# The opening of a fused attention and convolution block on one core: where the norm weights are loaded, the order of ScalarE's casts, and the order of V's first two token tiles

## The chip, the core and the metric

The kernel runs on one core of a Trainium2 chip. The metric is the device time of one execution in microseconds. Each number of the profile belongs to a single profiled execution.

The engines have short names here, as in the profile: PE is TensorE (matrix products and transposes), PEld its weight loads, DVE is VectorE, ACT is ScalarE, POOL is GpSimd, and SP is SyncE, which in this kernel only issues DMAs. Each engine takes its instructions in the order in which they stand on it.

## What is computed

One layer of a hybrid decoder block on 1024 tokens of width 1024, all in float32:

```python
h = rms_norm(x, attn_norm_w[l])
proj = h @ w_in[l]
q, k, v, u, g = jnp.split(proj, splits, axis=-1)
...
a = diff_attention(q[0], q[1], k[0], k[1], v, lam, rel_bias)
y_a = (rms_norm(a, subln_w[l]) * (1.0 - lam_init)).reshape(B, S, ATTN_WIDTH) @ w_proj_attn[l]
c = causal_depthwise_conv(u_a * jax.nn.sigmoid(u_b), conv_w[l], conv_b[l])
y_b = jax.nn.silu(layer_norm(c, conv_ln_w[l], conv_ln_b[l])) @ w_proj_conv[l]
g_a, g_b = jnp.split(jax.nn.sigmoid(g + gate_b[l]), 2, axis=-1)
x = x + (g_a * y_a + g_b * y_b) @ w_out[l]
h = rms_norm(x, ffn_norm_w[l])
gt, up = jnp.split(h @ w_gate_up[l], 2, axis=-1)
x = x + (jax.nn.silu(gt) * up) @ w_down[l]
```

This case is about the first 60 us: the first `rms_norm`, the transposes that bring its result into the form that PE needs, and the first columns of `h @ w_in`.

## The kernel before

**Split products.** PE works in a format of shorter mantissa. So every float32 operand is split into a high part (a cast, `split_hi`, ACT, L120) and a low part (the operand less its high part, `split_lo`, DVE, L125), and a product is three matmuls: high by high, low by high, high by low. `hT_hi` and `hT_lo` are the two parts of the normalised, transposed x: 8 channel blocks (k = 0 to 7) by 1024 tokens.

**The opening, by token tiles.** A token tile is 128 tokens, i = 0 to 7. For each of them:

- `xload` (L189) fetches its two halves g = 0, 1 of 512 channels, 256 KB each.
- `squares_of` (ACT, L652) forms the sums of squares. Tile 0 goes its own way in `x_first`: one half's squares on ACT, the other's on DVE.
- `roots` turns sums into 1/rms: a first step on DVE (L646), the square root on ACT (L616), then five small steps on DVE (L617 to L621).
- `scale_x` (DVE, L667) multiplies each half by 1/rms and by the norm weights `wb`. These are `attn_norm_w`, broadcast to 128 partitions by two DMAs of 256 KB (L194).
- `turn_x` (PE, L673) transposes a half, four transposes into a PSUM buffer of two; `hi_x` (ACT, L120) and `lo_x` (DVE, L125) put it into `hT_hi` and `hT_lo`.

**V's weights.** 512 columns of V come in four pieces k = 0 to 3 of 512 KB (`v_load`, L821), each with two channel blocks. `w_hi(k)` (ACT) and `w_lo(k)` (DVE) split them. Indices 4 and 5 of the same helpers are the weights of the first U columns, whose two buffers are those of V's pieces 0 and 1, so `u_load` (L828) waits for `w_lo(0)` and `w_lo(1)`. `v_terms` (PE, L688) issues the matmuls of a token tile: 24 of 128x512, namely 8 channel blocks by three products, into one PSUM bank `o`. `TERMS` goes through the blocks with three products each; `halves[g]` are the eight products of four blocks with the weights' high part. `v_out` casts and splits the sum (ACT, DVE) and stores both parts.

**What sets the order.** Where `in_order(...)` stands around a block, each named engine runs the instructions of the block in the order of the program text. There is one such block for V's token tile 0, one for tile 1, one for tile 2, and then blocks for the first U columns. Outside them a planner may move instructions ahead, and does so with the loads and splits of later weights. Here the text's order on an engine matters: an instruction that waits holds up all behind it on its engine. Before the change the norm weights go out on ACT's DMA queue, while x and V's weights go out on SP's. At most eight of these DMAs are under way; a ninth waits for the first to land.

**After the opening** come the rest of V, U, Q, K and the gates with the depthwise convolution on DVE beside them, the attention, the projections, and the channel mixer.

Of the kernel before, what the change touches and what calls it, by code (L numbers as in the profile page):

```python
# [57 lines left out]
def kernel(  # L58
# [27 lines left out]
    nc = tc.nc  # L86
# [25 lines left out]
    def nm(s):  # L112
        uid[0] += 1
        return f"{s}_{uid[0]}"

    def f32(ap):
        return ap.bitcast(F32)

    def split_hi(dst, src):
        act.copy(dst, src)  # L120
# [3 lines left out]
    def split_lo(dst, src, hi):  # L124
        last_lo[0] = dve.tensor_tensor(dst, src, f32(hi), op=ALU.subtract).ins  # L125
# [13 lines left out]
    def pg():  # L139
        npg[0] += 1  # L140
        p_, tag = pgs[npg[0] % len(pgs)]
        return p_.tile([P, 512], F32, tag=tag, name=nm("pg"))
# [48 lines left out]
    xload(0, 0)  # L191
    xload(0, 1, nc.scalar)
    for g in range(2):
        nc.scalar.dma_start(  # L194
            wb[:, 512 * g : 512 * (g + 1)], attn_norm_w[:, 512 * g : 512 * (g + 1)].to_broadcast([P, 512])
        )

# [485 lines left out]
    def v_terms(o, terms, w, i, first, last):  # L683

        ts = slice(i * P, (i + 1) * P)
        for n_, (k, a_, b_) in enumerate(terms):
            l_, r_ = (hT_hi, hT_lo)[a_][:, k, ts], w[k // 2][b_][:, k % 2, :]
            last_mm[0] = pe.matmul(  # L688
                o[:], l_, r_, start=first and n_ == 0, stop=last and n_ == len(terms) - 1
            ).ins  # L690

    def v_out(j, i, o):
        vh = ap.tile([P, 512], F32R, tag="vh", name=nm("vh"))
        vl = ap.tile([P, 512], F32R, tag="vl", name=nm("vl"))
        split_hi(vh[:], o[:])
        split_lo(vl[:], o[:], vh[:])
        for src, dst in ((vh, v_hi[j]), (vl, v_lo[j])):
            nc.sync.dma_start(dst[i * P : (i + 1) * P, :], f32(src[:]))

    TERMS = [(k, a_, b_) for k in range(NKT) for a_, b_ in ((0, 0), (0, 1), (1, 0))]  # L700
# [113 lines left out]
    def opening():  # L814


        raws = [wraw(), wraw()] + [ap.tile([P, 1024], F32, tag="vraw", name=nm("vraw"), bufs=2) for k in range(2)]
        uraw = [wraw(), wraw()]

        def v_load(k):  # L820
            nc.sync.dma_start(  # L821
                raws[k][:].rearrange("p (k c) -> p k c", c=512),
                win[2 * k * P : 2 * (k + 1) * P, V0 : V0 + 512].rearrange("(k p) c -> p k c", p=P),
            )

        def u_load(z):
            c0 = (U0 + D, U0)[z]
            nc.sync.dma_start(  # L828
                uraw[z][:].rearrange("p (k c) -> p k c", c=P),
                win[:, c0 : c0 + P].rearrange("(k p) c -> p k c", p=P),  # L830
            )

        def x_load(i):
            for g in range(2):
                xload(i, g)

        tiles = [vtiles() for k in range(4)] + [wtiles() for z in range(2)]
        raw6 = raws + uraw

        def w_hi(k):  # L840
            split_hi(tiles[k][0][:], raw6[k][:])

        def w_lo(k):
            split_lo(tiles[k][1][:], raw6[k][:], tiles[k][0][:])

        w = [[t_[:].rearrange("p (k c) -> p k c", c=512) for t_ in tiles[k]] for k in range(4)]
        uw = [[t_[:].rearrange("p (k c) -> p k c", c=P) for t_ in tiles[4 + z]] for z in range(2)]
        E_ = mybir.EngineType
        R, PT_ = {}, {}

        def turn_x(i, g):
            PT_[i, g] = x_turn(i, g)

        def hi_x(i, g):
            x_place(i, g, PT_[i, g], False)

        def lo_x(i, g):
            x_place(i, g, PT_[i, g], True)

        def squares_of(i, n):  # L860
            ss = sm.tile([P, 2], F32, tag="ss", name=nm("ss"))
            for e in range(n):
                x_squares(i + e, ss[:, e : e + 1])
            return ss

        def roots(i, n, ss):
            r = rstd_of(ss[:, :n], n, 1.0 / D)
            for e in range(n):
                R[i + e] = r[:, e : e + 1]

        def scale_x(i):
            for g in range(2):
                x_scale(i, R[i], g)

        with in_order(E_.PE, E_.Activation, E_.DVE, E_.SP):
            v_load(0)
            v_load(1)
            x_load(1)
            v_load(2)
            v_load(3)  # L880
            for i in range(2, NT):
                x_load(i)
            R[0] = x_first()
            scale_x(0)
            w_hi(0)
            turn_x(0, 0)
            hi_x(0, 0)
            turn_x(0, 1)
            lo_x(0, 0)
            w_hi(1)  # L890
            hi_x(0, 1)
            lo_x(0, 1)
            w_lo(0)
            ss = squares_of(1, 1)
            w_lo(1)
            u_load(0)
            u_load(1)
            roots(1, 1, ss)
            w_hi(2)
            scale_x(1)  # L900
            w_hi(3)
            w_lo(2)
            w_lo(3)
            o = pg()
            halves = [[(k, a_, 0) for a_ in range(2) for k in range(4 * g, 4 * g + 4)] for g in range(2)]
            v_terms(o, halves[0], w, 0, True, False)
            v_terms(o, halves[1], w, 0, False, False)
            v_terms(o, [(k, 0, 1) for k in range(4)], w, 0, False, False)
            turn_x(1, 0)
            hi_x(1, 0)  # L910
            lo_x(1, 0)
            turn_x(1, 1)
            ss = squares_of(2, 2)
            hi_x(1, 1)
            lo_x(1, 1)
            v_terms(o, [(k, 0, 1) for k in range(4, 8)], w, 0, False, True)
            roots(2, 2, ss)
            scale_x(2)
            v_out(0, 0, o)
        yield  # L920
        with in_order(E_.PE, E_.Activation, E_.DVE, E_.SP):
            o = pg()
            v_terms(o, TERMS[:12], w, 1, True, False)
            for g in range(2):
                turn_x(2, g)
                hi_x(2, g)
                lo_x(2, g)
            scale_x(3)
            w_hi(4)
            ss = squares_of(4, 2)  # L930
            v_terms(o, TERMS[12:], w, 1, False, True)
            roots(4, 2, ss)
            v_out(0, 1, o)
        yield
        with in_order(E_.PE, E_.Activation, E_.DVE, E_.SP):
            o = pg()
            v_terms(o, TERMS[:12], w, 2, True, False)
            for g in range(2):
                turn_x(3, g)
                hi_x(3, g)  # L940
                lo_x(3, g)
            w_lo(4)
            scale_x(4)
            w_hi(5)
            w_lo(5)
            ss = squares_of(6, 2)
            v_terms(o, TERMS[12:], w, 2, False, True)
            roots(6, 2, ss)
            scale_x(5)
            v_out(0, 2, o)  # L950
        yield

        def norm_of(i, nxt):
            for g in range(2):
                turn_x(i, g)
                hi_x(i, g)
                lo_x(i, g)
            if nxt is not None:
                scale_x(nxt)

        sg = {}

        def u_half(z, sb, amid):
            o = gemm_T(uw[z], hT_hi, hT_lo, sb, amid)
            if z == 0:
                sg[sb] = wp.tile([P, 512], F32, tag="sg", name=nm("sg"), bufs=2)
                act.activation(sg[sb][:], o[:], AF.Sigmoid)
            else:
                dve.tensor_tensor(sg[sb][:], o[:], sg[sb][:], op=ALU.mult)
                nc.sync.dma_start(u_d[0][:, sb * 512 : (sb + 1) * 512], sg[sb][:])  # L970

        with in_order(E_.PE, E_.Activation, E_.DVE):
            u_half(0, 0, lambda: norm_of(4, 6))
            norm_of(5, 7)
        yield
        with in_order(E_.PE, E_.Activation, E_.DVE):
            u_half(1, 0, lambda: norm_of(6, None))
            norm_of(7, None)
        yield
        with in_order(E_.PE, E_.Activation, E_.DVE):  # L980
            u_half(0, 1, None)
            vectors()
        yield
        with in_order(E_.PE, E_.Activation, E_.DVE):
            u_half(1, 1, None)
        bg.add([conv_load(0)])
        bg.add(conv_taps(0))
        yield
        yield from v_item(0, w, 3)
# [365 lines left out]
    for c in range(NE, NKT):  # L1355
        w = ws.next()
# [6 lines left out]
    for cl in ((0, 1, 2), (3, 4), (5, 6), (7,)):  # L1363
        pair = [(c, ws.next()) for c in cl]
        for sb in range(2):
            cs = slice(sb * 512, (sb + 1) * 512)
            for c, w in pair:
                g = gated(g_d[NKT + c], cs)
                ya = bp.tile([P, 512], F32, tag="ya", name=nm("ya"), bufs=4)
                nc.sync.dma_start(ya[:], ya_d[c][:, cs])  # L1370
                o = gemm_T(w, cT_hi, cT_lo, sb)
# [61 lines left out]
    for z, (c, ls) in enumerate(WO):  # L1433
        ts_ = [4 * l + i for l in ls for i in range(4)]
        o = {t_: wo_bank(t_) for t_ in ts_}
# [321 lines left out]
```

## Time and profile before

| | |
|---|---|
| time, median of 3 runs (lowest, highest) | 1768.91 us (1768.19, 1770.76) |
| the profiled execution: time, span from first to last instruction | 1769.82 us, 1768.0 us |
| PE busy | 1740.1 us, 98% of the span |
| DVE busy | 1273.1 us, 72% |
| ACT busy | 800.8 us, 45% |
| DMA | 275.29 MB, mean 156 GB/s |

A row of the timeline gives start and length in us, the engine, the line of the program, the operation, what it writes and reads, and how many instructions are merged into the row; in brackets stands how long the engine sat idle before and what ended that. In the names, `px` is the PSUM buffer of the transposes, `pg` that of products, `xt` a token tile of x, `anw_b` the norm weights, `vwh`/`vwl` V's split weights, `whi`/`wlo` other split weights, `xj` the squares' throw-away output, `vh`/`vl` the split V.

### The profile page before, as it was taken

Reading aid. Unit: us, or ns where it says so; the run is one execution under the profiler, and the core shown is the slowest. Engines: PE = TensorE matmul, PEld = TensorE weight load, DVE = VectorE, ACT = ScalarE, POOL = GpSimd, SP = SyncE. Lnnn points to the kernel's source line nnn. Section 1 sums busy time; section 2 is a strip of 40 time slices with the busy share of each in tenths; the row PEclk is TensorE's granted clock in tenths of the full one; section 3 lists DMA queues with packets and bytes.
Section 4 is the critical chain, followed back from the end, with each engine's and each line's share of the span. In section 5 each row is a group of like instructions: output and inputs, shape, how many; then the busy total and the mean of one; then the engine's idle time right before and its main releaser. Section 6 shows DMA issues by size and latency. Waiting matters only on the chain.

```text
span 1768.0 us, 25005 instructions
## 1 busy us (share of the span) xinstructions
PE 1740.1 (98%) x8983; PEld 1484.6 (84%) x8983; DVE 1273.1 (72%) x2171; ACT 800.8 (45%) x1883; POOL 19.6 (1%) x92
## 2 busy tenths in 40 slices
PE   6999999999999999999999999999999999999999
PEld 5778898998999998987788888878888888888887
DVE  6598888998898888885677534867667666665544
ACT  5221141557767776754457313633333333333332
POOL 0000000000000000000000000000000000000000
PEclk9999999999999999999999999999999999999999
DMA  6337334235443244341973544224544544697663
GB/s 231 107 125 232 131 111 115 70 104 138 120 141 105 82 125 145 97 147 60 339 261 108 167 166 143 90 90 152 171 159 148 177 153 148 202 357 250 214 214 131
DMA packets 251110, 275.29 MB, mean 156 GB/s; under 512 B 16505, under 2 KB 166050, under 8 KB 250986
## 3 DMA queue, kind: packets, MB, share of 16 engines
q1 hardware_dynamic: 249130, 267.47, 47.0%
q0 software_dynamic: 1280, 4.91, 0.9%
q10 hardware_dynamic: 576, 1.31, 0.3%
q8 instruction: 71, 1.16, 0.3%
q14 instruction: 53, 0.43, 0.1%
HBM read 176.59 MB, written 78.68 MB: 144 GB/s over the span
## 4 chain that ended last, share of the span: by engine, by line
PE 91%; DMA 3%; DVE 2%; ACT 2%; issue 1%; SPq 0%; DVEq 0%; ACTq 0%
PE acc L1611 19%; PE pg L153 14%; PE pg L154 14%; PE pg L155 14%; PE acc L497 12%; PE pg L688 4%; PE sc L1053 2%; PE sc L1052 2%; PE pT L1088 2%; PE wo L154 2%; PE wo L153 2%; PE wo L155 2%; PE pW L155 1%; PE pW L153 1%; PE pW L154 1%
## 5 line engine op out<-in xcount | busy, mean ns | idle before, releaser
L569 DVE SCALAR_TENSOR_TENSOR acc<-u,cw,acc 128x1024 f32<-128x1024 f32 x240 | 306.9, 1279 | 2.9
L153 PE MATMUL pg<-hT_hi,whi 128*128 128x512 f32 x512 | 201.7, 394 | 0.5 <-ACT hT_hi L120 0.2
L154 PE MATMUL pg<-hT_lo,whi 128*128 128x512 f32 x512 | 200.9, 392 | 0.0
L155 PE MATMUL pg<-hT_hi,wlo 128*128 128x512 f32 x512 | 200.7, 392 | 0.0
L120 ACT CAST whi<-wraw 128x1024 fp32r<-128x1024 f32 x101 | 106.1, 1051 | 182.9 <-PE pg L154 99.5
L125 DVE TENSOR_TENSOR wlo<-wraw,whi 128x1024 fp32r<-128x1024 f32 x101 | 123.0, 1219 | 63.3 <-ACT whi L120 59.4
L125 DVE TENSOR_TENSOR wlo<-draw,whi 128x1024 fp32r<-128x1024 f32 x75 | 91.8, 1224 | 89.1 <-ACT whi L120 86.1
L153 PE MATMUL pg<-whi,hT_hi 128*128 128x256 f32 x512 | 146.0, 285 | 0.3 <-ACT jk L756 0.3
L155 PE MATMUL pg<-whi,hT_lo 128*128 128x256 f32 x512 | 145.8, 285 | 0.0
L154 PE MATMUL pg<-wlo,hT_hi 128*128 128x256 f32 x512 | 145.5, 284 | 0.0
L120 ACT CAST whi<-draw 128x1024 fp32r<-128x1024 f32 x75 | 79.1, 1055 | 129.5 <-PE acc L497 122.6
L1059 ACT ACTIVATE E<-E,mn 128x256 f32<-128x256 f32 (+7 forms) x128 | 99.6, 780 | 45.9 <-DVE mn L1054 44.7
L497 PE MATMUL acc<-wlo,whi 128*128 128x512 f32 x308 | 119.8, 389 | 0.0
L497 PE MATMUL acc<-whi,wlo 128*128 128x512 f32 x308 | 119.8, 389 | 0.0
L153 PEld LDWEIGHTS pg<-hT_hi,whi 128*128 128x128 f32 x512 | 96.2, 188 | 20.5 <-ACT sgg L603 0.7
L155 PEld LDWEIGHTS pg<-hT_hi,wlo 128*128 128x128 f32 x512 | 96.2, 188 | 19.1
L154 PEld LDWEIGHTS pg<-hT_lo,whi 128*128 128x128 f32 x512 | 96.2, 188 | 19.0 <-issue 0.6
L153 PEld LDWEIGHTS pg<-whi,hT_hi 128*128 128x128 f32 x512 | 97.7, 191 | 2.2 <-ACT jk L756 1.0
L154 PEld LDWEIGHTS pg<-wlo,hT_hi 128*128 128x128 f32 x512 | 97.7, 191 | 1.3
L155 PEld LDWEIGHTS pg<-whi,hT_lo 128*128 128x128 f32 x512 | 97.7, 191 | 0.4
L1611 PE MATMUL acc<-h_hi,whi 128*128 128x512 f32 x240 | 93.4, 389 | 0.0
L1611 PE MATMUL acc<-h_lo,whi 128*128 128x512 f32 x240 | 93.4, 389 | 0.0
(280 smaller groups left out, 4191.1 us busy)
## 6 DMA issues: line engine op xcount, KB each, us to landing
wraw<-in_w_gate_up_dram SPq DMA_DIRECT2D x44, 512.0 KB, 4.8
wraw<-in_w_in_dram SPq DMA_DIRECT2D x38, 512.0 KB, 4.2
qs<-qs SPq DMA_DIRECT2D x96, 128.0 KB, 2.3
wd<-in_w_down_dram SPq DMA_DIRECT2D x44, 256.0 KB, 3.2
tdT<-wd SPq DMA_DIRECT2D x88, 128.0 KB, 4.5
draw<-sdS SPq DMA_DIRECT2D x44, 256.0 KB, 2.6
draw<-tdT SPq DMA_DIRECT2D x44, 256.0 KB, 4.3
wraw<-in_w_in_dram SPq DMA_DIRECT2D x32, 256.0 KB, 3.4
```

What stands on the lines that cost most here:

```text
L120: act.copy(dst, src)
L125: last_lo[0] = dve.tensor_tensor(dst, src, f32(hi), op=ALU.subtract).ins
L153: pe.matmul(o, lh, rh, start=start, stop=False)
L154: pe.matmul(o, lh, rl, start=False, stop=False)
L155: last_mm[0] = pe.matmul(o, ll, rh, start=False, stop=stop).ins
L497: m = pe.matmul(o[s_][i][:], l_[:, ts], r_[:, 512:], start=start and j + y_ == 0, stop=j == n - 1 and y_ == 2, skip_group_check=not start,)
L569: dve.scalar_tensor_tensor(acc[0][:], us[c][:, t : t + S], cw[:, c, t : t + 1], acc[0][:], op0=ALU.mult, op1=ALU.add)
L688: last_mm[0] = pe.matmul(o[:], l_, r_, start=first and n_ == 0, stop=last and n_ == len(terms) - 1).ins
L1052: pe.matmul(o[:, :w], qh[:, qs], k, start=True, stop=False)
L1053: last_mm[0] = pe.matmul(o[:, :w], ql[:, qs], k, start=False, stop=True).ins
L1059: act.activation(e[:, :nk], e[:, :nk], AF.Exp, bias=mn[:, j : j + 1], scale=-1.0, accum_out=l[:, j : j + 1])
L1611: pe.matmul(o[:], a_[x_][:, k, :], b_[y_][:, k, :], start=start and k + x_ + y_ == 0, stop=k == 3 and x_ == 1, skip_group_check=not start,)
```

## The change

Three things, all in the opening:

1. The two DMAs of the norm weights are issued on SP's queue, ahead of V's weights, instead of on ACT's queue.
2. The order of ACT's work changes: the casts of V's pieces 0 and 1 both stand ahead of those of token tile 0, the squares of tiles 2 and 3 ahead of tile 1's casts, the cast of U's first weights ahead of a root. DVE's order changes with it: one weight split instead of two ahead of tile 1's root, and the scaling of tiles 4 and 5 ahead of U's low weights and of a root.
3. On PE, token tile 1's products start before tile 0's are complete: after the 16 products of tile 0 with the weights' high part come tile 1's transposes, then tile 0's and tile 1's remaining products in turns. Tile 1's block of the order is merged into tile 0's.

```diff
@@ -191,7 +191,7 @@
     xload(0, 0)
     xload(0, 1, nc.scalar)
     for g in range(2):
-        nc.scalar.dma_start(
+        nc.sync.dma_start(
             wb[:, 512 * g : 512 * (g + 1)], attn_norm_w[:, 512 * g : 512 * (g + 1)].to_broadcast([P, 512])
         )
@@ -883,54 +883,50 @@
             R[0] = x_first()
             scale_x(0)
             w_hi(0)
-            turn_x(0, 0)
-            hi_x(0, 0)
-            turn_x(0, 1)
-            lo_x(0, 0)
             w_hi(1)
-            hi_x(0, 1)
-            lo_x(0, 1)
+            for g in range(2):
+                turn_x(0, g)
+                hi_x(0, g)
+                lo_x(0, g)
             w_lo(0)
             ss = squares_of(1, 1)
+            roots(1, 1, ss)
+            w_hi(2)
+            w_hi(3)
+            scale_x(1)
             w_lo(1)
+            w_lo(2)
             u_load(0)
             u_load(1)
-            roots(1, 1, ss)
-            w_hi(2)
-            scale_x(1)
-            w_hi(3)
-            w_lo(2)
-            w_lo(3)
-            o = pg()
+            ss = squares_of(2, 2)
+            o, o1 = pg(), pg()
             halves = [[(k, a_, 0) for a_ in range(2) for k in range(4 * g, 4 * g + 4)] for g in range(2)]
+            lows = [[(k, 0, 1) for k in range(4 * g, 4 * g + 4)] for g in range(2)]
             v_terms(o, halves[0], w, 0, True, False)
             v_terms(o, halves[1], w, 0, False, False)
-            v_terms(o, [(k, 0, 1) for k in range(4)], w, 0, False, False)
-            turn_x(1, 0)
-            hi_x(1, 0)
-            lo_x(1, 0)
-            turn_x(1, 1)
-            ss = squares_of(2, 2)
-            hi_x(1, 1)
-            lo_x(1, 1)
-            v_terms(o, [(k, 0, 1) for k in range(4, 8)], w, 0, False, True)
+            for g in range(2):
+                turn_x(1, g)
+                hi_x(1, g)
+                lo_x(1, g)
+            w_lo(3)
             roots(2, 2, ss)
             scale_x(2)
-            v_out(0, 0, o)
-        yield
-        with in_order(E_.PE, E_.Activation, E_.DVE, E_.SP):
-            o = pg()
-            v_terms(o, TERMS[:12], w, 1, True, False)
+            v_terms(o, lows[0], w, 0, False, False)
+            v_terms(o1, halves[0] + halves[1], w, 1, True, False)
+            v_terms(o, lows[1], w, 0, False, True)
+            v_terms(o1, lows[0], w, 1, False, False)
             for g in range(2):
                 turn_x(2, g)
                 hi_x(2, g)
                 lo_x(2, g)
+            v_out(0, 0, o)
             scale_x(3)
+            ss = squares_of(4, 2)
+            v_terms(o1, lows[1], w, 1, False, True)
             w_hi(4)
-            ss = squares_of(4, 2)
-            v_terms(o, TERMS[12:], w, 1, False, True)
             roots(4, 2, ss)
-            v_out(0, 1, o)
+            v_out(0, 1, o1)
+        yield
         yield
@@ -939,14 +935,14 @@
                 turn_x(3, g)
                 hi_x(3, g)
                 lo_x(3, g)
+            scale_x(4)
             w_lo(4)
-            scale_x(4)
             w_hi(5)
             w_lo(5)
             ss = squares_of(6, 2)
             v_terms(o, TERMS[12:], w, 2, False, True)
+            scale_x(5)
             roots(6, 2, ss)
-            scale_x(5)
             v_out(0, 2, o)
         yield
```

## The prediction

> **What bounds the kernel now.** First the busy time by stretches (a row gives the length, then the busy time of each engine, the granted clock, the share and rate of the DMA engines).
>
> ```profile
> 0.00:60.00 60.00, 45.10 (x206) 35.79 (x207) 36.95 (x75) 29.66 (x50) 2.32 (x12) 1.00 0.58 196
> 60.00:400.00 340.00, 339.65 (x1806) 291.65 (x1804) 286.97 (x374) 108.77 (x313) 7.12 (x24) 1.00 0.40 126
> ```
>
> TensorE (PE) is busy 339.65 of the 340 us after the opening, but only 45.10 of the first 60. So a microsecond that PE saves in the opening should reach the end, and what is saved on any other engine counts only through PE. Next PE's own timeline of the opening (start, length, count; in brackets the idle time before and who ended it):
>
> ```profile
> 8.46 1.09 PE L673 MATMUL px<-ident,xt 128*128 128x128 f32 x4 [8.46 <-DVE xt L667]
> 11.83 2.06 PE L688 MATMUL pg<-vwh,hT_hi 128*128 128x512 f32 x4
> 13.68 1.91 PE L688 MATMUL pg<-vwh,hT_lo 128*128 128x512 f32 x4
> 17.08 2.17 PE L688 MATMUL pg<-vwh,hT_hi 128*128 128x512 f32 x4 [1.49 <-ACT vwh L120]
> 19.04 1.81 PE L688 MATMUL pg<-vwh,hT_lo 128*128 128x512 f32 x4
> 20.69 1.09 PE L688 MATMUL pg<-vwl,hT_hi 128*128 128x512 f32 x4
> 21.61 1.03 PE L673 MATMUL px<-ident,xt 128*128 128x128 f32 x8
> 28.49 1.29 PE L673 MATMUL px<-ident,xt 128*128 128x128 f32 x8 [2.17 <-DVE xt L667]
> 46.25 1.25 PE L673 MATMUL px<-ident,xt 128*128 128x128 f32 x8 [0.99 <-DVE hT_lo L125]
> 54.97 0.50 PE L153 MATMUL pg<-hT_hi,whi 128*128 128x512 f32 x1 [0.24 <-ACT hT_hi L120]
> ```
>
> The 46.25 row holds token tile 5's transposes. After them PE idles 0.24 us once and then no more. So my measure of the opening is the start of that row. Two more things stand here. Four matmuls starting at 19.04 take 1.65 us until the next group, four starting at 20.69 take 0.92: 0.41 against 0.23 us each. PE runs at half speed until about 20.6. (The clock column says 1.00 throughout; I go by the spacing.) And PE waits for ScalarE's (ACT's) casts at 17.08 and for tile 2's scaling at 28.49. Why that scaling is late is read from the other two engines:
>
> ```profile
> 7.57 0.75 DVE L667 SCALAR_TENSOR_TENSOR xt<-xt,r,anw_b 128x512 f32<-128x512 f32 x1 [1.07 <-DMA anw_b<-in_attn_norm_w_dram]
> 10.26 0.75 DVE L667 SCALAR_TENSOR_TENSOR xt<-xt,r,anw_b 128x512 f32<-128x512 f32 x1 [1.94 <-DMA anw_b<-in_attn_norm_w_dram]
> 22.86 0.69 DVE L125 TENSOR_TENSOR hT_lo<-px,hT_hi 128x512 fp32r<-128x512 f32 x1 [2.09 <-ACT hT_hi L120]
> 25.57 0.69 DVE L125 TENSOR_TENSOR hT_lo<-px,hT_hi 128x512 fp32r<-128x512 f32 x1 [2.01 <-ACT hT_hi L120]
> 33.62 0.17 DVE L646 TENSOR_SCALAR v<-ss 128x2 f32<-128x2 f32 x1 [1.16 <-ACT xj L652]
> 37.56 1.22 DVE L125 TENSOR_TENSOR wlo<-wraw,whi 128x1024 fp32r<-128x1024 f32 x1
> 45.51 1.28 DVE L125 TENSOR_TENSOR hT_lo<-px,hT_hi 128x512 fp32r<-128x512 f32 x2
> ```
>
> ```profile
> 7.63 1.05 ACT L120 CAST vwh<-wraw 128x1024 fp32r<-128x1024 f32 x1 [2.09 <-DMA wraw<-in_w_in_dram]
> 9.59 0.59 ACT L120 CAST hT_hi<-px 128x512 fp32r<-128x512 f32 x1 [0.91 <-PE px L673]
> 10.75 1.05 ACT L120 CAST vwh<-wraw 128x1024 fp32r<-128x1024 f32 x1 [0.57 <-DMA wraw<-in_w_in_dram]
> 12.70 1.06 ACT L652 ACTIVATE xj<-xt 128x1024 bf16<-128x1024 f32 x1
> 15.89 0.20 ACT L616 ACTIVATE t<-v 128x1 f32<-128x1 f32 x1 [2.04 <-DVE v L646]
> 16.00 1.98 ACT L120 CAST vwh<-vraw 128x1024 fp32r<-128x1024 f32 x2
> 22.25 0.59 ACT L120 CAST hT_hi<-px 128x512 fp32r<-128x512 f32 x1 [4.28 <-PE px L673]
> 24.97 0.57 ACT L120 CAST hT_hi<-px 128x512 fp32r<-128x512 f32 x1
> 26.37 0.20 ACT L616 ACTIVATE t<-v 128x2 f32<-128x2 f32 x1 [0.83 <-DVE v L646]
> ```
>
> VectorE (DVE) idles 2.09 and 2.01 us in tile 1, because ACT's two casts of tile 1 (22.25 and 24.97) come late and stand on both sides of the two squares. From 37.56 to the 45.51 row DVE is the bound: PE's last real wait, 0.99 us, is for the low part of tile 4 (45.51).
>
> **The change, step by step.** Its own durations are those above. Back to back, a DVE instruction costs about 0.08 us less than its length (two low parts of 0.69 take 1.28), so I count 1.13 for a weight split, 1.33 for two scalings, 1.2 for two low parts, and 1.5 for the root with its small steps (41.15 to 42.54 in the rows that follow, with ACT's answer in it).
>
> ```profile
> 41.15 0.16 DVE L646 TENSOR_SCALAR v<-ss 128x2 f32<-128x2 f32 x1
> 42.38 0.16 DVE L621 TENSOR_TENSOR r<-r,t 128x2 f32<-128x2 f32 x1
> 43.78 0.68 DVE L125 TENSOR_TENSOR vl<-pg,vh 128x512 fp32r<-128x512 f32 x1
> ```
>
> PE's eight transposes in the chain of waits, and DMA by stretches:
>
> ```profile
> 50.25 0.87 PE px L673 x8
> ```
>
> ```profile
> 0.00:4.00 4.00, 0.00 (x0) 0.00 (x0) 0.00 (x0) 1.28 (x1) 1.66 (x10) 1.00 0.49 162
> 4.00:6.00 2.00, 0.00 (x0) 0.00 (x0) 1.22 (x6) 0.93 (x3) 0.00 (x0) 1.00 0.95 241
> 6.00:8.00 2.00, 0.00 (x0) 0.00 (x0) 0.86 (x4) 0.37 (x1) 0.00 (x0) 1.00 0.96 329
> 8.00:10.00 2.00, 1.09 (x4) 0.72 (x4) 0.32 (x1) 1.09 (x2) 0.00 (x0) 1.00 0.98 357
> 10.00:12.00 2.00, 0.94 (x5) 0.94 (x6) 1.35 (x2) 1.22 (x2) 0.00 (x0) 1.00 1.06 407
> ```
>
> *Norm weights in SP's queue.* Two issues leave ACT's queue, which then is free anyway, and enter SP's ahead of V's four weights and all other x tiles. The issues behind them go out later; that is hidden, since the DMA engines are 0.95 busy and more from 4 us on. Without that cover it would cost an issue each. Both scalings of tile 0 can then start from 6.5 and 7.3 instead of 7.57 and 10.26, and the eight transposes end near 9.1 instead of after 11.01. That alone is worth nothing, because of the next edit. V's first weights land later, near 8.5 (7.63 now), as the norm weights no longer come beside them but before. For the second weights the sum of what is ahead is unchanged: x tile 0, norm weights, V's first and second weights, 2.1 MB, and they land at 10.75 now. The windows above moved 2.5 MB by 10 us and reach 2.1 MB at 8.9, so the landing lags by up to 1.85; with a part of that, the earliest is 9.6. If the 0.52 MB of norm weights go at the slowest rate in those rows (162 against 407 GB/s), 1.9 us are added. I take 10.5, nearest to the measured 10.75, with 9.6 and 12.4 as ends.
>
> *Casts reordered on ACT.* The second weights' cast now stands ahead of both casts of tile 0. So tile 0's high part comes at 10.5 + 0.95 + 0.6 = 12.1, not 10.17, and PE's first matmul at 12.1 instead of 11.83: 0.3 us **lost**. Behind it queue tile 1's square, its root, and the third and fourth weights' casts. DVE does one weight split, not two, ahead of the root: two low parts from 12.1 to 13.3, the split to 14.5, the root's first step to 14.6. ACT's 2.04 us wait shrinks to about 0.9 and those casts run from 14.8 (16.00 now): 1.2 won. PE then needs them at 15.6 and finds them at 15.9: the 1.49 us hole becomes 0.3. Both squares of tiles 2 and 3 go ahead of tile 1's casts and end at 19.1, about when tile 1's transposes do (18.4 to 19.3); DVE's two idle times of tile 1, 4.1 us together, nearly go.
>
> *Two token tiles interleaved.* Between 12.1 and tile 2's transposes stand 44 matmuls and 8 transposes. At full speed that is 44 x 0.23 + 0.87 = 11.0 us. Half speed costs half of the time up to the switch. Now PE is continuously at work from 17.08 and the switch comes 3.5 us later; from 12.1 on it would come between 15.6 and, if the count must begin anew once, 19.1. I take 17.2: 2.5 us lost. With 0.3 of holes, tile 2's transposes start at 25.9 (28.49 now). Tile 2's scaling is ready at 24.8 (tile 1's low parts end near 21, then a split, the root and the scalings), so the wait of 2.17 us goes, with what PE has in tile 1 as its cover.
>
> The Trainium skill (TensorE: Matmul & The Clock Gate, Part 1) says that the clock rises after about 3.4 us of sustained work, counted in windows that run free of the kernel. The rows agree (17.08 to about 20.6). By the rule alone the switch lies anywhere in 15.5 to 18.9.
>
> *What is late next.* After tile 2's low parts DVE has no cover left: from 27.1 (1.2 behind the transposes' start: four of them take some 0.6 by the 28.49 row, ACT's cast 0.59) it does two low parts 1.2, tile 0's V low 0.6, two scalings 1.33, a root 1.5 plus 0.6 since ACT now casts U's weights ahead of it, V low 0.6, two low parts of tile 3 1.2, and then tile 4's scaling 1.33, moved ahead of U's low weights 1.2. These end at 36.7 (38.78 now). PE has finished V's third tile at 34.1 (28 matmuls and 16 transposes from 25.9) and U needs the low weights for its third matmul: a **new wait of some 2 us**, which gives back part of the gain. From there PE has 22 matmuls and 8 transposes (5.9 us) to tile 5's transposes, and DVE has a split 1.13, scalings 1.33, root 1.5, V low 0.6, a split of the next weights 1.13 and the low part 0.69, 6.4 together less overlap: 42.6 to 43 for both. PE's restart after a stop costs 0.2 (eight transposes took 1.25 at 46.25, 1.03 at 21.61). I take 42.8. Putting tile 5's scaling ahead of its root merely swaps two pieces of DVE's chain: nothing.
>
> **Sum:** 46.25 - 42.8 = 3.45 us. The profiled execution took 1769.82 us (span 1768.0), giving 1766.4; it stands 0.9 above the median of the runs, 1768.91. Against the median I predict **1765.5**. About 0.2% (3.5 us) can be told from no change, so the forecast lies on that border.
>
> **The rivals.** *More is won:* weights at 9.6 and the switch at 15.6 give 41.6, a gain of 4.7. The two later seams add to this:
>
> ```profile
> 820.00:823.00 3.00, 2.88 (x13) 2.48 (x12) 2.02 (x4) 1.87 (x6) 0.20 (x1) 0.50 0.57 190
> 823.00:826.00 3.00, 3.00 (x16) 3.00 (x15) 0.02 (x1) 0.53 (x3) 0.00 (x0) 0.50 0.00 0
> 1177.00:1181.00 4.00, 3.94 (x12) 2.81 (x11) 2.89 (x3) 2.04 (x3) 0.00 (x0) 0.59 0.76 217
> ```
>
> PE gets half the clock there, a price of 6 x 0.5 = 3.0 and 4 x 0.41 = 1.6 us. Shifted by 3.4 us, either seam may keep its clock: 1764 to 1761. Taken together 1763, chance 0.25.
>
> *Less is won:* the second weights land at 11.5 to 12.4, since the norm weights read by 128 partitions now hold up the queue (only 241 GB/s in 4 to 6 us speaks for it), or DVE's chain stretches: 1.0 to 1.9 us less, 1767. Chance 0.20.
>
> *Slower:* half speed stays. PE's new sequence is paced by casts, has holes at 15.6 and 16.8, and puts tile 1's transposes (18.4 to 19.3) inside the stretch that must count as busy; now it had only matmuls. Each us beyond 17.2 costs 0.5, so the change loses from 24.1 on. Two more stretches of 3.5 (17.08 to 20.6) end at 24.2; after a third, 27.7, tile 5 starts at 48.05: 1.8 slower, 1770.7. That transposes at 21.61 and 28.49 did not bring half speed back speaks against it. Chance 0.07. The Trainium skill (TensorE: Matmul & The Clock Gate, Part 4: PE-mode transpose) says that transposes do not count as work for the clock in the same way; no run here shows that yet.
>
> *No effect:* a planner's placement undoes the order. The order is tied by hand on four engines, so 0.03; 1768.9.
>
> **How the numbers follow.** Forecast 0.45 (1764.2 to 1767), rivals 0.25, 0.20, 0.07, 0.03. Faster by over 0.2%: 0.20 of the forecast's and nearly all of the first rival, 0.44. Slower by over 0.2%: 0.05, for half speed that stays still longer or seams that lose another window. Within: 0.51. The range goes from 1761.5 (first rival with one seam) to 1769.5.
>
> **What would show it.** Right: tile 0's transposes near 7.3; V's first matmul at 12.1; spacing 0.23 from about 17; no DVE wait over 0.5 us in tile 1; PE waiting some 2 us for U's low weights near 34.5 to 36.7; tile 5's transposes at 42 to 43.5. Wrong: a first matmul after 13, spacing 0.43 beyond 21, or a changed count of half-clock stretches at the seams, which would move the time without the opening.

## The result, and the profile after

| | before | after |
|---|---|---|
| median of 8 runs (lowest, highest) | 1770.14 us (1767.48, 1772.96) | 1765.73 us (1764.44, 1769.98) |
| ratio, 95% interval | | 0.9978 (0.9968 to 0.9989) |
| profiled execution: time, span | 1769.82, 1768.0 us | 1764.81, 1763.0 us |
| PE's first product of V | 11.83 us | 12.08 us |
| PE at full clock from (the trace's record of the clock) | 20.6 us | 15.3 us |
| start of token tile 5's transposes | 46.25 us | 43.01 us |

The changed kernel is faster, by 0.22% with an interval from 0.11% to 0.32%. The median of three runs on which the prediction was made, 1768.91, lay 1.2 below that of all eight.

The busy time by stretches of the changed kernel, with the columns of before:

```profile
0.00:60.00 60.00, 46.92 (x220) 37.34 (x221) 36.79 (x75) 28.97 (x50) 2.31 (x12) 1.00 0.58 196
60.00:400.00 340.00, 339.62 (x1817) 292.01 (x1816) 290.46 (x381) 112.28 (x327) 7.10 (x24) 1.00 0.41 128
```

From 60 to 400 us nothing has changed: PE is full. In the opening it has more work done by the same time. PE's timeline shows where:

```profile
7.60 2.22 PE L673 MATMUL px<-ident,xt 128*128 128x128 f32 x8 [7.60 <-DVE xt L667]
12.08 2.08 PE L688 MATMUL pg<-vwh,hT_hi 128*128 128x512 f32 x4 [2.27 <-ACT hT_hi L120]
13.96 1.70 PE L688 MATMUL pg<-vwh,hT_lo 128*128 128x512 f32 x4
16.73 0.73 PE L688 MATMUL pg<-vwh,hT_hi 128*128 128x512 f32 x2 [0.22 <-ACT vwh L120]
17.30 1.08 PE L688 MATMUL pg<-vwh,hT_lo 128*128 128x512 f32 x4
18.22 1.03 PE L673 MATMUL px<-ident,xt 128*128 128x128 f32 x8
25.47 1.03 PE L673 MATMUL px<-ident,xt 128*128 128x128 f32 x8
36.24 0.50 PE L155 MATMUL pg<-hT_hi,wlo 128*128 128x512 f32 x1 [2.03 <-DVE wlo L125]
43.01 1.26 PE L673 MATMUL px<-ident,xt 128*128 128x128 f32 x8 [0.59 <-DVE hT_lo L125]
```

From 12.08 to 34.2 us the longest hole is 0.22 us. Four matmuls starting at 17.30 take 0.92 until the transposes, so PE is at full speed there, some 5 us before the old kernel. Tile 2 (25.47) comes 3.02 us earlier. Then the new wait of 2.03 us for U's low weights stands at 36.24, and tile 5 is reached 3.24 us earlier. ACT and DVE show what lies behind this:

```profile
9.18 1.05 ACT L120 CAST vwh<-wraw 128x1024 fp32r<-128x1024 f32 x1 [3.58 <-DMA wraw<-in_w_in_dram]
10.50 1.05 ACT L120 CAST vwh<-wraw 128x1024 fp32r<-128x1024 f32 x1 [0.28 <-DMA wraw<-in_w_in_dram]
11.45 1.07 ACT L120 CAST hT_hi<-px 128x512 fp32r<-128x512 f32 x2
14.58 0.20 ACT L616 ACTIVATE t<-v 128x1 f32<-128x1 f32 x1 [1.01 <-DVE v L646]
14.69 1.99 ACT L120 CAST vwh<-vraw 128x1024 fp32r<-128x1024 f32 x2
18.86 1.08 ACT L120 CAST hT_hi<-px 128x512 fp32r<-128x512 f32 x2
```

```profile
7.90 0.75 DVE L667 SCALAR_TENSOR_TENSOR xt<-xt,r,anw_b 128x512 f32<-128x512 f32 x1 [0.44 <-DMA anw_b<-in_attn_norm_w_dram]
19.48 1.29 DVE L125 TENSOR_TENSOR hT_lo<-px,hT_hi 128x512 fp32r<-128x512 f32 x2
26.73 1.29 DVE L125 TENSOR_TENSOR hT_lo<-px,hT_hi 128x512 fp32r<-128x512 f32 x2 [2.07 <-ACT hT_hi L120]
30.98 0.17 DVE L617 RECIPROCAL r<-t 128x2 f32<-128x2 f32 x1 [0.87 <-ACT t L616]
34.97 2.35 DVE L125 TENSOR_TENSOR wlo<-wraw,whi 128x1024 fp32r<-128x1024 f32 x2
41.13 1.23 DVE L125 TENSOR_TENSOR wlo<-wraw,whi 128x1024 fp32r<-128x1024 f32 x1 [0.56 <-ACT whi L120]
```

Tile 1's two casts now run back to back at 18.86 (22.25 and 24.97 before), and DVE's two waits in tile 1 are gone: the row at 19.48 has no bracket.

The span shrank by 5.0 us, the opening by 3.24. Nothing in the opening's rows accounts for the rest. At the seam near 817 us PE's clock was halved for one stretch in this execution, for two in that of before (the rows at 820 and 823 in the prediction). The busy time by stretches of the changed kernel:

```profile
817.40:820.80 3.40, 3.18 (x16) 2.78 (x15) 1.51 (x3) 2.29 (x8) 0.20 (x1) 0.50 0.49 159
820.80:824.00 3.20, 3.20 (x23) 2.94 (x23) 0.00 (x0) 0.37 (x1) 0.00 (x0) 0.99 0.00 0
```

3.4 us of half clock saved are 1.7 us, and 3.24 + 1.7 = 4.9 of the 5.0.

### The profile page after: what moved, and what is told of

Same layout as the page of the kernel before. It is cut to its first block, busy times and chain, and to the rows that moved or that the text cites. A ratio compares the mean times of both kernels' runs of the same rounds, so it can differ in the third digit from the quotient of the medians.

```text
span 1763.0 us, 25003 instructions
## 1 busy us (share of the span) xinstructions
PE 1737.3 (99%) x8983; PEld 1481.9 (84%) x8983; DVE 1273.3 (72%) x2171; ACT 801.9 (45%) x1883; POOL 19.6 (1%) x92
## 4 chain that ended last, share of the span: by engine, by line
PE 92%; DVE 2%; DMA 2%; ACT 2%; issue 1%; SPq 0%; DVEq 0%; ACTq 0%
PE acc L1607 19%; PE pg L153 14%; PE pg L154 14%; PE pg L155 14%; PE acc L497 12%; PE pg L688 4%; PE sc L1049 2%; PE sc L1048 2%; PE pT L1084 2%; PE wo L154 2%; PE wo L153 2%; PE wo L155 2%; PE pW L153 1%; PE pW L155 1%; PE pW L154 1%
```

## The experiments

For each kernel the start of tile 5's transposes is read from its profile, as the end of the opening. It varies from one execution to the next with two things that no order sets, the landing of V's second weights and the clock, so the table has both beside it. Each profile is a single execution, so a few tenths of a microsecond mean little. The times of one kernel vary by 2.5 to 6 us, so the ratios alone separate little. The kernels were timed in three series (the changed kernel; the next four; the last four), each beside the kernel before, whose median was 1770.14, 1769.43 and 1768.93. So across series the ratios are to be compared, not the medians.

| kernel | median, us (runs) | ratio to before, 95% | first product | full clock | tile 2 | tile 5 |
|---|---|---|---|---|---|---|
| changed | 1765.73 (8) | 0.9978 (0.9968 to 0.9989) | 12.08 | 15.3 | 25.47 | 43.01 |
| queue_alone | 1768.98 (10) | 0.9996 (0.9987 to 1.0005) | 10.37 | 19.5 | 27.42 | 45.18 |
| queue_back | 1766.84 (10) | 0.9982 (0.9973 to 0.9992) | 12.25 | 16.9 | 25.63 | 44.02 |
| tiles_apart | 1767.10 (10) | 0.9984 (0.9975 to 0.9993) | 11.82 | 17.0 | 27.05 | 44.48 |
| casts_back | 1765.27 (8) | 0.9977 (0.9966 to 0.9987) | 10.66 | 20.2 | 26.76 | 44.03 |
| wlo4_first | 1766.61 (10) | 0.9984 (0.9975 to 0.9993) | 12.46 | 18.4 | 26.42 | 43.89 |
| squares_back | 1766.54 (10) | 0.9984 (0.9974 to 0.9993) | 11.12 | 14.8 | 25.27 | 43.07 |
| early_u | 1763.85 (5) | 0.9962 (0.9949 to 0.9974) | 11.36 | 15.8 | 24.75 | 39.62 |
| early_u_casts | 1763.06 (5) | 0.9962 (0.9950 to 0.9975) | 9.69 | 13.6 | 23.93 | 38.84 |

### The queue alone

```diff
 # on the kernel before
     for g in range(2):
-        nc.scalar.dma_start(
+        nc.sync.dma_start(
             wb[:, 512 * g : 512 * (g + 1)], ...
```

> The kernel before with the change's first part alone: the norm weights on SP's queue ahead of V's weights; all orders as before. Measure: start of token tile 5's transposes on PE (46.25 us before, 43.01 after). Theory (the orders win, the queue only makes tile 0's scaling early, and what it frees is behind other waits): 45.5 to 46.3, time 0 to 0.8 us less than before. Rival (the early norm weights are the gain): 43 to 44, 2.2 to 3.3 us less. Rival (the queue costs, V's first weights at 9.2 instead of 7.6): later than 46.5. The full clock of PE may come one stretch earlier or later than in the profile of before, which moves each figure by up to 1.5 us; it is read from the spacing of the matmuls.

The interval of the ratio contains 1: no gain can be told, and the rival that the early norm weights are the gain falls. In the profile tile 5 comes at 45.18, 1.07 earlier than before and 0.3 earlier than the theory's band. PE's timeline of this kernel shows that the waits of before are all still there:

```profile
10.37 2.16 PE L688 MATMUL pg<-vwh,hT_hi 128*128 128x512 f32 x4 [0.78 <-ACT hT_hi L120]
16.03 2.17 PE L688 MATMUL pg<-vwh,hT_hi 128*128 128x512 f32 x4 [1.79 <-ACT vwh L120]
27.42 1.29 PE L673 MATMUL px<-ident,xt 128*128 128x128 f32 x8 [2.20 <-DVE xt L667]
45.18 1.25 PE L673 MATMUL px<-ident,xt 128*128 128x128 f32 x8 [0.99 <-DVE hT_lo L125]
```

The first product is 1.5 us earlier, but the third weights' cast keeps PE waiting for 1.79 instead of 1.49, so only 1.05 of it is left at 16.03 (17.08 before).

### The queue put back

```diff
 # on the changed kernel
-        nc.sync.dma_start(
+        nc.scalar.dma_start(
             wb[:, 512 * g : 512 * (g + 1)], ...
```

> The changed kernel with the norm weights put back on ACT's queue. Theory: tile 0's transposes are late again (8.4 and 11), but PE's first product waits for the cast of V's second weights either way: first product at 12.3 (12.08 after), tile 5's transposes at 43.2 to 43.5, time within 0.5 us of the changed kernel. Rival (the queue is the gain): tile 5 at 45 or later, 2 us or more slower than the changed kernel.

Up to tile 2 the theory holds to 0.2 us: first product at 12.25, tile 2 at 25.63 (25.47 in the changed kernel). The time, too, cannot be told from that of the changed kernel (ratios 0.9982 and 0.9978, the intervals nearly the same). Tile 5 misses its band by 0.5, and the likely cause is another one. The busy time by stretches of this kernel shows a clock of 0.50 behind the new wait:

```profile
33.00:37.40 4.40, 2.38 (x11) 1.65 (x10) 4.40 (x7) 2.68 (x5) 0.00 (x0) 1.00 0.23 84
37.40:40.80 3.40, 3.40 (x11) 2.62 (x10) 2.91 (x10) 1.34 (x3) 0.00 (x0) 0.50 0.94 254
```

A wait of 2.02 us that ends at 36.39, for U's low weights and as long as that of the changed kernel, was followed here by 3.4 us at half clock.

### The two token tiles apart

```diff
 # on the changed kernel
-            v_terms(o1, halves[0] + halves[1], w, 1, True, False)
             v_terms(o, lows[1], w, 0, False, True)
+            v_terms(o1, halves[0] + halves[1], w, 1, True, False)
```

> The changed kernel with one line of PE's order moved: tile 0's products are finished before tile 1's begin; ACT and DVE as changed. Theory: PE waits for the fourth low weights, ready at 21.9, with nothing to do from 19.9: about 1.6 us lost; tile 2's transposes at 27.1 (25.47 after), tile 5's at 44.6, so half of the gain of the opening is gone. Rival (the order of casts is the gain, the interleave nothing): tile 5 at 43.0 to 43.3. Rival (the interleave is all): 46.

Tiles 2 and 5 come within 0.2 us of what the theory has. PE's timeline shows the hole, 1.30 us where 1.6 was expected:

```profile
21.93 0.73 PE L688 MATMUL pg<-vwl,hT_hi 128*128 128x512 f32 x2 [1.30 <-DVE vwl L125]
27.05 1.03 PE L673 MATMUL px<-ident,xt 128*128 128x128 f32 x8
44.48 1.25 PE L673 MATMUL px<-ident,xt 128*128 128x128 f32 x8 [0.49 <-DVE hT_lo L125]
```

Tile 2 comes 1.58 and tile 5 1.47 us later, a little under half of the opening's 3.24. Not all of this need be the order: the full clock came at 17.0 here, at 15.3 in the changed kernel. But queue_back, with the full clock at 16.9, had tile 2 at 25.63, so with nearly equal clocks the order is still worth 1.4 in the profiles. The ratios, 0.9984 against 0.9978, go the same way, but their intervals overlap.

### Tile 0's casts in their old place

```diff
 # on the changed kernel
             w_hi(0)
+            turn_x(0, 0)
+            hi_x(0, 0)
+            turn_x(0, 1)
+            lo_x(0, 0)
             w_hi(1)
-            for g in range(2):
-                turn_x(0, g)
-                hi_x(0, g)
-                lo_x(0, g)
+            hi_x(0, 1)
+            lo_x(0, 1)
```

> The changed kernel with tile 0's casts in their old place, that is between the casts of V's first and second weights. Theory: the new place costs 0.3 to 0.5 us; first product at 10.8 (12.08 after), tile 2's transposes at 25.1 (25.47), tile 5's at 42.5 to 42.8 (43.01); time 0.2 to 0.5 us less than the changed kernel. Rival (the new place is a part of the gain, because PE then starts without holes): tile 5 after 43.3.

The first product is at 10.66, as expected. But tile 5 is 1.0 later than in the changed kernel, so in this profile the rival has it. PE's timeline gives a hole of 0.65 us that the theory left out of account:

```profile
15.18 2.17 PE L688 MATMUL pg<-vwh,hT_hi 128*128 128x512 f32 x4 [0.65 <-ACT vwh L120]
18.86 1.69 PE L673 MATMUL px<-ident,xt 128*128 128x128 f32 x8
```

The eight transposes at 18.86 take 1.69 us, not 1.03: PE was still at half speed and came to full clock at 20.2 only, 9.5 us after its first product (3.2 in the changed kernel). The full clock came 4.9 us later, which at half speed costs some 2.45; less the 1.42 by which the first product was earlier this leaves 1.0, as measured. Over eight runs each the two kernels are alike, with ratios of 0.9977 and 0.9978. So no effect of the place of tile 0's casts on the time can be told: a first product 1.4 us earlier stands against a half speed that may last longer.

### U's low weights first again

```diff
 # on the changed kernel
-            scale_x(4)
             w_lo(4)
+            scale_x(4)
             w_hi(5)
```

> The changed kernel with U's first low weights put back ahead of the scaling of tile 4 on DVE: the order there as before the change. Theory (the 2.0 us wait of PE is where DVE's chain shows, not a cost of its own): the wait shrinks to 0.7 us, tile 5's transposes stay at 42.5 to 43.2, PE now waits some 2 us there instead, the time is within 0.5 us of the changed kernel. Rival (the wait is lost time): tile 5 at 41.5 or earlier, 1.3 to 2 us less than the changed kernel.

PE's timeline has the old wait cut and the next one grown:

```profile
35.86 0.50 PE L155 MATMUL pg<-hT_hi,wlo 128*128 128x512 f32 x1 [0.70 <-DVE wlo L125]
43.89 1.25 PE L673 MATMUL px<-ident,xt 128*128 128x128 f32 x8 [1.85 <-DVE hT_lo L125]
```

0.70 + 1.85 here, 2.03 + 0.59 in the changed kernel: 2.55 against 2.62. The wait moved, as the theory says, and the time did not fall. Tile 5 itself is 0.7 later than the theory's band, but the delay arose before the edited lines: tile 2 already came at 26.42, 0.95 later than in the changed kernel, with the first product at 12.46 and the full clock at 18.4 only. From tile 2 to tile 5 it is 17.47 us here and 17.54 in the changed kernel.

### The squares in their old place

```diff
 # on the changed kernel
-            ss = squares_of(2, 2)
             o, o1 = pg(), pg()
...
-            for g in range(2):
-                turn_x(1, g)
-                hi_x(1, g)
-                lo_x(1, g)
+            turn_x(1, 0)
+            hi_x(1, 0)
+            lo_x(1, 0)
+            turn_x(1, 1)
+            ss = squares_of(2, 2)
+            hi_x(1, 1)
+            lo_x(1, 1)
```

> The changed kernel with the squares of tiles 2 and 3 back between the two casts of tile 1 on ACT. Theory (tile 1's high part comes 2.3 us later and holds up tile 1's products, the root of tiles 2 and 3 and so tile 2): tile 2's transposes at 26.2 (25.47 after), tile 5's at 43.8 to 44.2 (43.01), 0.8 to 1.2 us slower than the changed kernel. Rival (the interleave on PE hides it): tile 5 within 0.3 of 43.0.

By the letter the rival has it: tile 5 at 43.07. But this execution's first product was 0.96 us earlier than the changed kernel's. Counted from the first product, tile 2 comes after 14.15 (13.39 in the changed kernel) and tile 5 after 31.95 (30.93), 0.8 and 1.0 later, as the theory says. The times (ratios 0.9984 and 0.9978, the intervals overlap) do not settle it. I take it as likely and not shown.

### DVE's chain shortened

```diff
 # early_u, on the changed kernel
             v_out(0, 0, o)
+            w_hi(4)
             scale_x(3)
+            w_lo(4)
             ss = squares_of(4, 2)
             v_terms(o1, lows[1], w, 1, False, True)
-            w_hi(4)
             roots(4, 2, ss)
-            v_out(0, 1, o1)
...
+            v_out(0, 1, o1)
             scale_x(4)
-            w_lo(4)
             w_hi(5)
+            scale_x(5)
             w_lo(5)
             ss = squares_of(6, 2)
             v_terms(o, TERMS[12:], w, 2, False, True)
-            scale_x(5)
-            roots(6, 2, ss)
             v_out(0, 2, o)
...
                 lo_x(i, g)
+            if i == 4:
+                roots(6, 2, ss)
             if nxt is not None:
```

> The changed kernel with DVE's chain shortened ahead of tile 5: U's first weights are cast and split before tile 4's root, tile 1's V parts are split after tile 3's casts, both scalings of tiles 4 and 5 stand ahead of U's second low weights, and the root of tiles 6 and 7 goes behind tile 4's low parts. Nothing is left out. Theory (DVE's chain is the last bound of the opening): PE waits under 0.8 us for U's weights, tile 5's transposes at 40.2 to 41, PE without a wait of 1 us after 13; 2 to 3 us less than the changed kernel, ratio to the kernel before about 0.9963. Rival (PE is the bound by then, DVE only follows): tile 5 at 42 or later. The later waits of PE at 816 and 1171 us stay as they are by both.

Tile 5 is reached at 39.62, 3.4 us earlier than in the changed kernel (0.7 of it by the earlier first product) and 0.6 earlier than the theory's band. After the first product PE's timeline has no wait over 0.25 us left up to 60 us:

```profile
11.36 2.08 PE L688 MATMUL pg<-vwh,hT_hi 128*128 128x512 f32 x4 [1.92 <-ACT hT_hi L120]
24.75 1.03 PE L673 MATMUL px<-ident,xt 128*128 128x128 f32 x8
35.60 1.03 PE L673 MATMUL px<-ident,xt 128*128 128x128 f32 x8
39.62 1.25 PE L673 MATMUL px<-ident,xt 128*128 128x128 f32 x8 [0.24 <-DVE hT_lo L125]
48.75 0.50 PE L153 MATMUL pg<-hT_hi,whi 128*128 128x512 f32 x1 [0.24 <-ACT hT_hi L120]
```

So DVE's chain was the last bound, and the ratio, 0.9962, is what was expected (0.9963). No kernel of the table has a lower one, but its interval (up to 0.9974) overlaps that of the changed kernel (from 0.9968), so the further gain is shown in the opening and not in the time. In the profiled execution only 0.7 of the 3.4 us reached the end (spans 1763.0 and 1762.3). Later waits of PE took a part of it. The one for a load of V near 522 us was 1.40 us (0.43 in the changed kernel):

```profile
522.72 0.39 PE L155 MATMUL pW<-ph,vl 128*128 128x256 f32 x1 [1.40 <-DMA vl<-v_lo]
```

Two waits for DVE that end at 1188 and 1532 us, 1.1 us together, have no counterpart in the changed kernel.

With tile 0's casts in their old place besides:

> The kernel early_u with tile 0's casts also in their old place, between the casts of V's first and second weights. Theory: first product at 10.7, tile 5's transposes 0.3 to 0.5 us earlier than in early_u if the full clock of PE comes at the same time, 39.8 to 40.6; but a hole of some 0.7 us near 15 can put off the full clock by one stretch of 3.4 us, which costs up to 1.7 us. So the time within 1 us of early_u, either way. Rival (holes do not matter to the clock): always earlier than early_u.

Tile 5 comes at 38.84, 0.8 earlier than in early_u and 1.0 earlier than the band. The first product was at 9.69, 1.0 earlier than expected, and the full clock at 13.6, as the hole of 0.65 that ends at 14.21 was only beginning. So this execution cannot separate the theory from the rival. The ratio is the same, 0.9962. Both kernels are faster than the kernel before, and their ratios are lower than the changed kernel's, with intervals that overlap its; between them nothing can be told.

## Why the prediction was right, point by point

- **The bound.** That only PE counts and that the opening ends at tile 5's transposes held: in the profiled pair 3.24 us of the opening and 1.7 of a seam make up the span's 5.0. It need not hold for every change: of the 3.4 us that early_u won in the opening, 0.7 reached the end of its profiled execution.
- **Norm weights in SP's queue, worth nothing by themselves.** Held as far as the times tell: ratio 0.9996 alone, no difference that can be told without them. V's second weights were cast from 10.50; 10.5 was taken. V's first weights were cast from 9.18, 0.7 later than forecast, and tile 0's transposes ended at 9.8 instead of 9.1; neither cost anything, as PE's first product waited for casts that stand behind that of the second weights.
- **Casts reordered.** First product 12.08 (12.1 forecast), third and fourth weights' casts from 14.69 (14.8), the hole 0.22 (0.3), at 16.73. All within 0.1. That the early place of the weights' cast is a loss of 0.3 us was only half of it: it also leaves PE without a hole of 0.65 us behind its first product, which in casts_back kept PE at half speed for longer. Over many runs the two cannot be told apart.
- **Interleave.** Tile 2 at 25.47 against 25.9. The mis-sized term is the switch to full clock: 15.3, not 17.2, worth 1.0 us of half speed, and 0.2 before the range of 15.5 to 18.9 that stands in the prediction. That was luck: the other four kernels whose first product waits in the same way came to full clock 3.7 to 5.9 us after it, this one 3.2. About half of it was lost again, because PE at full speed ran into the casts: the four matmuls from 15.77 took 1.53 us up to the next group, where 0.92 is full speed. The interleave alone is worth about 1.4 us in the profiles.
- **The new wait.** 2.03 us at 36.24, where some 2 us at 34.5 to 36.7 were forecast. As said there, it gives back part of the gain. That it is DVE's chain and not a price of its own is shown by wlo4_first and early_u.
- **Tile 5.** 43.01 against 42.8. DVE waited 0.56 us for the cast of the next weights, which the sum did not have.
- **The total.** 3.24 us in the opening against 3.45; median 1765.73 against 1765.5. The forecast lay on the border of 0.2%, and so does the ratio. That the median comes within 0.3 us of the forecast is in part luck: the forecast started from a median of three runs that lay 1.2 low, and the drop between the medians of eight is 4.4 us, not 3.4. The surplus fits the seam's 1.7 in the profiled pair, but no run shows where it lies in the other executions.
- **The rivals.** Half speed that stays: the opposite came, the full clock earlier than before. That transposes would not count as work for the clock is not borne out: in casts_back the last 3.41 us before the full clock (16.78 to 20.19) held 2.1 us of matmuls and 1.3 of transposes, while 2.77 us of work in the stretch before had not been enough (the rows stand in the last section). More is won: the early switch came, the early weights did not. The seams: they did move in the profiled pair, by 1.7 us, so one of the signs of being wrong, a changed count of half-clock stretches, came beside the right opening. At that seam the two profiles with the old orders have 6.8 us of half clock; of the eight with the new ones five have 3.4 and three 6.8. So it is neither shown nor ruled out that the change has a part in this. Less won by late weights: not in this execution. Executions of kernels with the same early order had their first product anywhere from 11.12 to 12.46, so by an estimate from these starts this alone can move the end of the opening by up to 1.3 us.

## What to carry to other kernels

On an engine that issues in order, put first what the saturated engine will need next, and let long work for a later stage (squares, roots, scalings) fill the gaps. Interleave two independent tiles where the second operand of the first is still being made. Of these, the interleave's worth is shown in the profiles here, that of the squares' place is likely only. When a new wait appears after such a change, follow its engine on to the next wait: here moving the wait won nothing (wlo4_first), and shortening the chain behind it won 3.4 us of the opening (early_u).

## What the runs showed of the hardware that was not expected

**Holes decide when PE gets its full clock.** In every trace the recorded changes of the clock lie whole multiples of 3.413 us apart: 20.60, 819.32, 826.14, 1177.72 and 1181.13 in the kernel before. The Trainium skill (TensorE: Matmul & The Clock Gate, Part 1) has the clock counted in free-running windows of some 3.4 us; the traces agree. Counted back from the full clock in such stretches, the last one ahead of it had PE busy for 94 to 100% in all ten traces, and none before that for more than 81%. Over the whole traces every stretch at half clock in which PE was busy for 89% or more was followed by full clock, and none with 88% or less was. Two stretches of casts_back, with the hole of 0.65 us and without it, and the last one of the changed kernel (the length comes first, then PE's busy time; the clock column says 1.00 because the record of the clock starts with its first change):

```profile
13.36:16.78 3.42, 2.77 (x7) 1.41 (x7) 2.98 (x10) 2.79 (x4) 0.00 (x0) 1.00 1.05 404
16.78:20.19 3.41, 3.41 (x13) 2.82 (x12) 2.10 (x2) 1.74 (x5) 0.00 (x0) 1.00 1.04 397
```

```profile
11.88:15.29 3.41, 3.21 (x8) 2.48 (x8) 2.89 (x7) 2.40 (x6) 0.00 (x0) 1.00 1.05 405
```

So a hole of 0.65 us can spoil a stretch, and where the first product falls in its stretch is luck. Where holes of 0.65 us or more fell behind the first products at half speed, the full clock came 8.8 us (before, hole 1.49), 9.1 (queue_alone, 1.79) and 9.5 (casts_back, 0.65) after the first product; with holes of 0.23 us at most, after 3.2 to 5.9 (the other kernels).

**A wait of 2 us can halve the clock.** The same wait of 2.02 to 2.03 us was followed by 3.4 us at a clock of 0.50 in queue_back and by none in the changed kernel. Counted in the same stretches, the wait of queue_back (34.37 to 36.39) lay wholly in one of them, 33.95 to 37.37, in which PE was busy for 1.40 us. That of the changed kernel was cut by the border at 35.78, and the emptier stretch still had 1.85 us of work. In the ten traces half clock followed every stretch with PE busy for 41% or less; from 44 to 50% it followed in one case and not in the others, and above that never. The Trainium skill (TensorE: Matmul & The Clock Gate, Why this matters for your kernels) calls for gaps of PE of no more than about 3 us; the measured 2.02 us is less, and was enough, so here the measurement decides. In the profiles 3.4 to 10.2 us behind PE's first full clock were at half clock. These halvings are a part of the spread of the times: of the 21 runs of the kernel before in the third series, the five with a mean granted clock of 0.996 took 1770.5 us on average, the fifteen with 0.997 or 0.998 1768.6.
